# Three vector-matrix products of layer 0 issued in single steps instead of in three bursts

## The chip, the cores and the metric

The kernel runs on one core of a Trainium2 chip, in one launch. The metric is the time of an execution on the device, in microseconds (us). The engines are named as in the profile: PE (TensorE, matrix products; PEld is its weight load), DVE (VectorE), ACT (ScalarE), POOL (GpSimd) and SP (SyncE, here only the queue that issues the transfers from HBM).

## The reference, cut to what matters

Two layers, each an attention-like mixer and an MLP, on x of 1024 tokens by 1024 columns, all in float32. Ahead of each layer, six vectors of 1024 are made from the one conditioning vector c:

```
cond = silu(c)
mod  = cond @ w_ada[l] + b_ada[l]          # 6 * 1024
shift_a, scale_a, gate_a, shift_f, scale_f, gate_f = split(mod, 6)
h = rms_norm(x) * (1 + scale_a) + shift_a
x = x + gate_a * mixer(h)                  # gated linear attention and latent attention
h = rms_norm(x) * (1 + scale_f) + shift_f
x = x + gate_f * (relu(h @ w_up)**2 @ w_down)
```

The vectors are numbered 0 to 5 here and called modulations. The change concerns 2 (gate_a), 3 (shift_f) and 4 (scale_f) of layer 0. None of them is needed before the mixer's output projection, which stands far behind the work that is spoken of here.

## The kernel before, in words

Activations lie transposed, columns on partitions, in two halves (A and B) of 512 tokens. Float32 products are made as three matmuls of a high and a low part each. So each weight block of 512 KB is loaded into a ring slot (SP queue), its high part is cast (ACT or DVE, L307), its low part subtracted (POOL or DVE, L308), and PE uses both.

All large buffers are slots of 4 KB per partition of one pool of 51, the ring. A slot that is given back goes to the end of a first-in-first-out list, and the next request takes the head of the list (class `Arena`). A load into a slot may be issued only when the last reader of its previous tenant is done, and SP issues its transfers in one fixed order.

The stages of a layer are tokens of the string PROGRAM, walked in order at build time, once for each layer. For half A and then half B: v0, v1, g0, g1 (value and gate projections), L (latent projection, with latent_rest behind it), Q or TA/QA and TB/QB (queries and keys, and the latent's rest), W (the seven-level scores of gated linear attention: PE L928 and DVE L954 to L989), O (their output); R makes the rotary tables: a chain of small DVE steps in one slot `ang`, that ends with ACT's sine and cosine (L551 to L556). The tile framework takes the dependencies of this walk and sets from them, and from a planned time for each engine, the order in which each engine gets its instructions. The engines then run each its own list in order, with semaphores between them.

One modulation is `ada_steps` (L240): for each of 8 blocks of w_ada a load of 512 KB (L245) and one DVE step over 128x1024 that multiplies it by an entry of cond and adds it up (L254 the first, L256 the others). One load is requested a step ahead of its use. The last step also makes eight PE transposes of the sum (L263) and four short DVE operations (L266, L267), with one more each for modulation 4. `ada` (L236) runs all eight steps at once; token Xm calls it.

Names in the rows: s is a ring tile, ps_x, ps_s, ps_m, ps_g are PSUM banks, tmp a small buffer, colsv and mod hold columns of vectors, cs the constants. L609 to L611 (L607 to L609 in the changed kernel) are the three matmuls of a value or gate projection.

Of the kernel before, what the change touches and what calls it, by code (L numbers as in the profile page):

```python
# [34 lines left out]


PROGRAM = (
# [3 lines left out]
).split()  # L41
# [85 lines left out]
def hybrid_kernel(  # L127
# [17 lines left out]
    R = lambda a: a.bitcast(F32R)  # L145
# [86 lines left out]
    def mcol(l, m, d):  # L232
        k = l * 48 + m * 8 + d
        return mod[:, k:k + 1]

    def ada(l, m):  # L236
        for _ in ada_steps(l, m):
            pass

    def ada_steps(l, m, tag=lambda: "x"):  # L240
        acc = AR.alloc()
# [77 lines left out]
    def ahead(n):  # L319
        while ustate["pos"] < min(n, len(units)) and len(AR.free_list) >= 5:  # L320
            prep()
# [19 lines left out]
    for l in range(DEPTH):  # L341
# [10 lines left out]
        for tok in PROGRAM:  # L352
            kind, rest = tok[0], tok[1:]
# [228 lines left out]
    def rope(dst, src, i, hf, room):  # L582
        C = ropeC[i][:, hf * 4:hf * 4 + 4, :]
        Sn = ropeS[i][:, hf * 4:hf * 4 + 4, :]
        m1 = room[:, 0:256].rearrange("p (t f) -> p t f", t=4)
        m2 = room[:, 256:512].rearrange("p (t f) -> p t f", t=4)
        G.tensor_tensor(m1, src, C, op=ALU.mult)
        G.tensor_tensor(m2[:, :, 0:32], src[:, :, 32:64], Sn[:, :, 0:32], op=ALU.mult)
        G.tensor_tensor(m2[:, :, 32:64], src[:, :, 0:32], Sn[:, :, 32:64], op=ALU.mult)
        G.tensor_tensor(dst[:, :, 0, :], m1, m2, op=ALU.add)  # L590
        G.tensor_tensor(dst[:, :, 1, :], m1, m2, op=ALU.add)


    wg = cp.tile([32, 256], F32, name="wg")
# [20 lines left out]
    def layer_mixer(l, hA, make_hB):  # L615
# [498 lines left out]
        def flush():  # L1114
            while pending:
                pending.pop(0)()
# [20 lines left out]
        for tok in PROGRAM:  # L1137
            kind, rest = tok[0], tok[1:]
            hf = "AB".index(rest[0]) if rest and rest[0] in "AB" else None
            if kind == "L":  # L1140
                latents(hf)
            elif kind == "H":
                hsb[1] = (hsb[1] or []) + make_hB(rest)
            elif kind == "R":
                if l == 0:
                    rope_angles()
                rope_tables(l)
            elif kind == "E":
                if l == 0:
                    enter(1)  # L1150
            elif kind == "T":
                latent_rest(hf)
            elif kind == "Q":
                queries_keys(hf)
            elif kind == "W":
                gla_scores(hf)
            elif kind == "v":
                values(hf, int(rest[1]))
            elif kind == "g":
                gates(hf, int(rest[1]))  # L1160
            elif kind == "O":
                gla_out(hf)
            elif kind == "M":
                mix_split(int(rest))
            elif kind in "uU":
                up(tok)
            elif kind == "a":
                attend(int(rest[0]), int(rest[1]))
            elif kind == "F":
                flush()  # L1170
            elif kind == "=":
                tags = TAGS[rest]
            elif kind == "X":
                if l == 0:
                    ada(0, int(rest))
            elif kind == "P":
                ahead(ustate["pos"] + int(rest))
            elif kind == "D":
                project(0, int(rest), mix)
                if int(rest) == 7:  # L1180
                    AR.free(*mix[0])
            elif kind == "N":
                norm_out(0)
# [274 lines left out]
```

## Time and profile before

| what | value |
|---|---|
| three runs | 2352.49, 2353.1, 2366.69 us (median 2353.1) |
| profiled execution | 2356.47 us, its span 2354.4 us |
| PE busy | 2236.2 us (95%) |
| DVE busy | 1810.4 us (77%) |
| ACT busy | 1141.1 us (48%) |
| POOL busy | 453.5 us (19%) |
| one percent of the median | 23.5 us |

The span is that from the first instruction of the profiled execution to its last; 2.07 us of its time lie around it. A busy share is that of the whole span. An idle time in square brackets, as `[3.05 <-DVE s L256]`, stands just ahead of the row that it belongs to, with the operation that ended it.

### The profile page before, as it was taken

The numbers are of one execution on the slowest core, as the hardware profiler recorded it, in microseconds if no ns is written. First come the engines' busy times: TensorE is split into PE (matmuls) and PEld (weight loads), VectorE is DVE, ScalarE is ACT, GpSimd is POOL, SyncE is SP. The second block draws the span as 40 slices with busy tenths as digits, with TensorE's granted clock in tenths as the row PEclk, the third lists the DMA queues.
The fourth block names the chain that finished last, engine by engine and source line by source line (L and its number), as shares of the span: only waits on it lengthen the run. The fifth ranks groups of instructions, "written<-read, shape, count | busy, mean of one in ns | idle before, by whom it ended". The sixth has DMA issues, their size and how long they took to land.

```text
span 2354.4 us, 30787 instructions
## 1 busy us (share of the span) xinstructions
PE 2236.2 (95%) x11784; PEld 1897.1 (81%) x11784; DVE 1810.4 (77%) x2453; ACT 1141.1 (48%) x1764; POOL 453.5 (19%) x326
## 2 busy tenths in 40 slices
PE   6999999899999998998989999899999999999999
PEld 4788888788788876887878889788888878887887
DVE  5897867857888888989995757786674767877894
ACT  3364746534732383433444556575366217733432
POOL 2452642420030000000063355333102000000000
PEclk8999999999999999999999999999999999999999
DMA  9633100136668655765641211003454564375562
GB/s 345 205 97 99 55 27 10 46 125 212 199 206 274 217 167 174 249 225 197 239 131 45 70 51 41 10 10 100 144 169 124 180 202 146 110 237 189 163 212 81
DMA packets 244855, 340.51 MB, mean 145 GB/s; under 512 B 11078, under 2 KB 166884, under 8 KB 244708
## 3 DMA queue, kind: packets, MB, share of 16 engines
q1 hardware_dynamic: 244160, 338.08, 44.2%
q8 instruction: 92, 1.51, 0.3%
q10 hardware_dynamic: 548, 0.48, 0.1%
q14 instruction: 55, 0.45, 0.1%
HBM read 317.54 MB, written 20.97 MB: 144 GB/s over the span
## 4 chain that ended last, share of the span: by engine, by line
PE 63%; DVE 12%; DMA 7%; ACT 2%; issue 2%; POOL 1%; SPq 0%; DVEq 0%; ACTq 0%; POOLq 0%
PE ps_m L162 8%; PE ps_m L163 7%; PE ps_m L161 7%; PE ps_s L162 5%; PE ps_s L163 5%; PE ps_s L161 5%; PE ps_g L163 4%; PE ps_g L162 4%; PE ps_g L161 4%; DMA s<-in_w_mlp_down_dram 3%; PE ps_x L163 2%; PE ps_x L162 2%; PE ps_x L161 2%; DMA s<-in_w_mlp_up_dram 2%; DMA s<-in_w_ada_dram 1%
## 5 line engine op out<-in xcount | busy, mean ns | idle before, releaser
L307 ACT CAST s<-s 128x1024 fp32r<-128x1024 f32 (+2 forms) x306 | 315.2, 1035 | 465.5 <-DVE s L304 275.7
L162 PE MATMUL ps_m<-s,s 128*128 128x512 f32 (+3 forms) x1084 | 411.1, 380 | 15.2 <-DVE s L1292 14.2
L308 POOL TENSOR_TENSOR s<-s,s 128x1024 fp32r<-128x1024 f32 (+2 forms) x90 | 222.7, 2481 | 1044.9 <-DVE s L307 524.1
L161 PE MATMUL ps_m<-s,s 128*128 128x512 f32 (+3 forms) x1084 | 408.6, 381 | 8.6 <-ACT s L1291 5.4
L163 PE MATMUL ps_m<-s,s 128*128 128x512 f32 (+3 forms) x1084 | 408.3, 377 | 0.2 <-DVE s L308 0.2
L308 DVE TENSOR_TENSOR s<-s,s 128x1024 fp32r<-128x1024 f32 (+1 forms) x224 | 272.5, 1227 | 55.6 <-ACT s L307 47.6
L161 PE MATMUL ps_s<-s,s 128*128 128x512 f32 (+5 forms) x800 | 306.4, 387 | 6.6 <-ACT s L724 6.1
L163 PE MATMUL ps_s<-s,s 128*128 128x512 f32 (+5 forms) x800 | 305.3, 383 | 1.5 <-DVE s L308 1.5
L162 PE MATMUL ps_s<-s,s 128*128 128x512 f32 (+5 forms) x800 | 305.2, 382 | 0.5 <-DVE s L748 0.5
L304 DVE TENSOR_TENSOR s<-s,s 128x1024 f32<-128x1024 f32 x160 | 196.9, 1233 | 122.1 <-DMA s<-in_w_mlp_up_dram 77.6
L162 PEld LDWEIGHTS ps_m<-s,s 128*128 128x128 f32 x1084 | 206.4, 190 | 55.9 <-DVE s L1292 17.7
L161 PEld LDWEIGHTS ps_m<-s,s 128*128 128x128 f32 x1084 | 205.6, 190 | 46.5 <-ACT s L1291 7.4
L1291 ACT CAST s<-s 128x1024 fp32r<-128x1024 f32 x140 | 146.7, 1051 | 192.8 <-DVE s L1289 57.2
L163 PEld LDWEIGHTS ps_m<-s,s 128*128 128x128 f32 x1084 | 206.0, 190 | 35.8 <-DVE s L308 0.6
L162 PE MATMUL ps_g<-s,s 128*128 128x512 f32 (+1 forms) x506 | 195.0, 386 | 1.6 <-DVE s L1292 1.6
L161 PE MATMUL ps_g<-s,s 128*128 128x512 f32 (+1 forms) x506 | 194.6, 388 | 0.8 <-DVE s L1338 0.8
L163 PE MATMUL ps_g<-s,s 128*128 128x512 f32 (+1 forms) x506 | 194.3, 387 | 0.8 <-DVE s L308 0.8
L1292 DVE TENSOR_TENSOR s<-s,s 128x1024 fp32r<-128x1024 f32 x140 | 173.5, 1244 | 13.8 <-ACT s L1291 10.8
L161 PEld LDWEIGHTS ps_s<-s,s 128*128 128x128 f32 x800 | 150.8, 189 | 37.0 <-ACT s L724 8.7
L163 PEld LDWEIGHTS ps_s<-s,s 128*128 128x128 f32 x800 | 151.4, 189 | 30.9 <-DVE s L308 1.9
L162 PEld LDWEIGHTS ps_s<-s,s 128*128 128x128 f32 x800 | 151.6, 190 | 27.6 <-DVE s L748 0.7
L162 PE MATMUL ps_x<-s,s 128*128 128x512 f32 (+3 forms) x362 | 124.1, 344 | 0.0
(332 smaller groups left out, 4412.6 us busy)
## 6 DMA issues: line engine op xcount, KB each, us to landing
s<-in_w_mlp_up_dram SPq DMA_DIRECT2D x192, 512.0 KB, 4.9
s<-in_w_mlp_down_dram SPq DMA_DIRECT2D x192, 512.0 KB, 4.3
s<-in_w_ada_dram SPq DMA_DIRECT2D x80, 512.0 KB, 4.8
s<-in_w_in_dram SPq DMA_DIRECT2D x48, 512.0 KB, 3.9
s<-in_w_ada_dram SPq DMA_DIRECT2D x32, 256.0 KB, 4.6
xd<-s SPq DMA_DIRECT2D x16, 512.0 KB, 6.1
s<-in_w_out_dram SPq DMA_DIRECT2D x16, 512.0 KB, 4.5
s<-xd SPq DMA_DIRECT2D x16, 512.0 KB, 3.5
```

The lines of the kernel that those rows point to most:

```text
L161: PE.matmul(o, lh, rh, start=start, stop=False)
L162: PE.matmul(o, lh, rl, start=False, stop=False)
L163: PE.matmul(o, ll, rh, start=False, stop=stop)
L304: V.tensor_tensor(raw[:, :n], raw[:, :n], u.second[:, :n], op=ALU.add if u.sign > 0 else ALU.subtract)
L307: (V.tensor_copy if u.eng[-2] == "v" else S.copy)(R(u.hi[:, :n]), raw[:, :n])
L308: (V if u.eng[-1] == "v" else G).tensor_tensor(R(u.lo[:, :n]), raw[:, :n], u.hi[:, :n], op=ALU.subtract)
L1291: S.copy(R(hi), t)
L1292: V.tensor_tensor(R(lo), t, hi, op=ALU.subtract)
```

## The change

The token X2, X3 and X4 each ran a whole modulation. Now the token Xn takes n steps from one generator that runs through modulations 2, 3 and 4 one after the other. Twelve tokens X2 stand between the stages of the mixer, from behind `=1` up to gB1: 24 steps, as many as before. The helper `ada` is gone. Layer 1 takes none, as before.

```diff
 PROGRAM = (
-    "vA0 E gA0 X2 R LA Ha =1 TA QA X3 Hb vA1 WA gA1 OA LB QB TB X4 gB0 WB gB1 u00 P1 vB0 u01 a00 P1 "
+    "vA0 E gA0 R LA Ha =1 X2 TA X2 QA X2 Hb vA1 X2 WA X2 gA1 X2 OA X2 LB X2 QB X2 TB X2 gB0 X2 WB X2 gB1 u00 P1 vB0 u01 a00 P1 "
...
-    def ada(l, m):
-        for _ in ada_steps(l, m):
-            pass
...
+    ada_work0 = (None for m in (2, 3, 4) for _ in ada_steps(0, m))
...
             elif kind == "X":
                 if l == 0:
-                    ada(0, int(rest))
+                    for _ in range(int(rest)):
+                        next(ada_work0)
```

Lines 240 to 590 of the kernel before are four lines further up in the changed one, later ones two. The tiles of the ring are numbered differently in the two, since the requests come in another order.

The first place is PE's list at the transposes of modulation 2 (L263 before, L259 now). Before, they stand within the latent projection of half A (128x464 matmuls):

```order
L161 MATMUL ps_s<-s_106_823,s_73_405 128x464
L161 MATMUL ps_m<-s_106_823,s_73_405 128x464
L161 MATMUL ps_s<-s_106_823,s_73_405 128x464
L263 MATMUL ps_x<-cs,s_91_729 128x128 x8
L162 MATMUL ps_s<-s_107_824,s_73_405 128x464
L163 MATMUL ps_s<-s_106_823,s_73_405 128x464
```

In the changed kernel they stand two stages later, between the halves of value projection vA1 and the first of the scores (L926):

```order
L607 MATMUL ps_s<-s_132_1072,s_39_298 128x256
L608 MATMUL ps_s<-s_133_1073,s_39_298 128x256
L609 MATMUL ps_s<-s_132_1072,s_39_298 128x256
L259 MATMUL ps_x<-cs,s_112_928 128x128 x3
L607 MATMUL ps_m<-s_135_1104,s_71_395 128x256
L607 MATMUL ps_s<-s_135_1104,s_71_395 128x256
L259 MATMUL ps_x<-cs,s_112_928 128x128
L926 MATMUL ps_g<-s_157_1331,s_127_1036 128x128
```

Those of modulation 3 move from ahead of the scores of half A to behind its latent stage LB, those of modulation 4 behind projection gB0.

The second place is DVE's list at the end of the rotary angles. Before:

```order
L551 TENSOR_SCALAR s_100_770<-s_100_770 128x256
L553 TENSOR_SCALAR s_100_770<-s_100_770 128x256
L554 TENSOR_TENSOR s_100_770<-s_100_770 128x256
L579 SCALAR_TENSOR_TENSOR s_102_806<-sinT,grp 128x8x32 x2
L839 COPY s_79_424<-ps_x 16x512
L555 TENSOR_SCALAR s_100_770<-s_100_770 128x256
L857 TENSOR_REDUCE ssq<-s_123_997 128x2 x3
L392 TENSOR_SCALAR rs_v<-ssq 128x4 x3
```

In the changed kernel (L551 there is L555 of before, L837 is L839, L252 is L256):

```order
L551 TENSOR_SCALAR s_91_729<-s_91_729 128x256
L252 SCALAR_TENSOR_TENSOR s_112_928<-s_114_931,cond,s_112_928 128x1024
L855 TENSOR_REDUCE ssq<-s_117_960 128x2 x3
L252 SCALAR_TENSOR_TENSOR s_112_928<-s_115_934,cond,s_112_928 128x1024
L303 CAST s_132_1072<-s_131_1070 128x1024
L855 TENSOR_REDUCE ssq<-s_118_965 128x2 x3
L252 SCALAR_TENSOR_TENSOR s_112_928<-s_124_1029,cond,s_112_928 128x1024
L388 TENSOR_SCALAR rs_v<-ssq 128x4 x3
L837 COPY s_79_424<-ps_x 16x512
```

Three steps of modulation 2 now stand between the last of the angles and the copy (L837) that PE's decay product waits for, and block s_114_931 of the first of them is loaded into the slot in which the angles (s_91_729) lay.

The third place is SP's list around the first block of gate projection gB0, which is s_200_1980 in both. Before:

```order
L292 DMA s_189_1881<-in_w_in_dram 128x8x128
L292 DMA s_197_1948<-in_w_in_dram 128x8x128
L292 DMA s_192_1911<-in_w_in_dram 128x8x128
L292 DMA s_200_1980<-in_w_in_dram 128x4x256
L245 DMA s_221_2176<-in_w_ada_dram 128x1024
L245 DMA s_218_2168<-in_w_ada_dram 128x1024
```

In the changed kernel:

```order
L288 DMA s_248_2578<-in_w_in_dram 128x4x256
L288 DMA s_245_2524<-in_w_in_dram 128x4x256
L241 DMA s_231_2309<-in_w_ada_dram 128x1024
L241 DMA s_232_2312<-in_w_ada_dram 128x1024
L288 DMA s_200_1980<-in_w_in_dram 128x4x256
L241 DMA s_244_2500<-in_w_ada_dram 128x1024
```

The block was row 87 of SP's list and is now row 103. It comes behind the two rows ahead of it in w_in of later use (s_248, s_245) and behind two blocks of modulation 4. Its slot is now that of a tile which the output stage of half A reads to its end (PE L1085 there).

## Rows read from the trace of the kernel before

**Rows 1.** The page's busy times of each engine over the span.
```profile
PE 2236.2 (95%) x11784; PEld 1897.1 (81%) x11784; DVE 1810.4 (77%) x2453; ACT 1141.1 (48%) x1764; POOL 453.5 (19%) x326
```
**Rows 2.** Stretches: us, PE PEld DVE ACT POOL busy, TensorE clock, DMA share.
```profile
50.00:100.00 50.00, 45.55 (x278) 42.15 (x279) 41.80 (x56) 22.15 (x36) 15.67 (x7) 0.90 0.61 216
...
150.00:200.00 50.00, 43.36 (x273) 40.14 (x272) 43.90 (x58) 26.41 (x43) 18.04 (x14) 0.93 0.30 84
200.00:250.00 50.00, 50.00 (x276) 43.04 (x275) 32.30 (x62) 24.98 (x43) 17.25 (x16) 0.97 0.40 123
```
**Rows 3.** Waits of PE, 45 to 460 us: in total, times, longest.
```profile
PE ps_x L263 <- DVE s L256: 6.6, 2, 3.6
```
**Rows 4.** Timeline of PE at the first burst: start, us, operation, [idle before].
```profile
89.78 1.09 PE L263 MATMUL ps_x<-cs,s 128*128 128x128 f32 x8 [3.05 <-DVE s L256]
...
91.03 0.59 PE L163 MATMUL ps_s<-s,s 128*128 128x464 f32 x1
91.42 0.59 PE L161 MATMUL ps_s<-s,s 128*128 128x464 f32 x1
...
94.38 0.37 PE L162 MATMUL ps_s<-s,s 128*128 128x464 f32 x1
94.58 0.38 PE L161 MATMUL ps_m<-s,s 128*128 128x464 f32 x1
```
**Rows 5.** Timeline of PE at the second burst.
```profile
154.69 1.07 PE L263 MATMUL ps_x<-cs,s 128*128 128x128 f32 x8 [3.55 <-DVE s L256]
...
155.76 0.42 PE L609 MATMUL ps_m<-s,s 128*128 128x256 f32 x1
155.98 0.42 PE L610 MATMUL ps_m<-s,s 128*128 128x256 f32 x1
...
160.24 0.28 PE L610 MATMUL ps_m<-s,s 128*128 128x256 f32 x1
160.36 0.28 PE L611 MATMUL ps_m<-s,s 128*128 128x256 f32 x1
```
**Rows 6.** Stretches of 5 us at the first burst, columns as in rows 2.
```profile
85.00:90.00 5.00, 1.95 (x11) 1.44 (x10) 5.00 (x6) 2.70 (x4) 1.50 (x2) 1.00 0.00 0
90.00:95.00 5.00, 5.00 (x21) 4.40 (x20) 5.00 (x7) 1.08 (x3) 1.96 (x1) 0.66 0.00 0
```
**Rows 7.** Timeline of DVE at the end of the rotary angles.
```profile
114.43 0.27 DVE L555 TENSOR_SCALAR s<-s 128x256 f32<-128x256 f32 x1
117.45 1.21 DVE L857 TENSOR_REDUCE ssq<-s 128x2 f32<-128x512 f32 x3 [2.75 <-ACT s L855]
...
120.51 0.17 DVE L395 SCALAR_TENSOR_TENSOR rs_a<-rs_y 128x12 f32<-128x12 f32 x1 [1.64 <-ACT rs_y L394]
```
**Rows 8.** Timeline of ACT at the same place.
```profile
114.73 0.42 ACT L556 ACTIVATE cosT<-s 128x256 f32<-128x256 f32 x1 [2.42 <-DVE s L555]
```
**Rows 9.** Transfers: landing of L245's blocks, then issues of the page (KB, us).
```profile
DMA to landing us min/median/max: 3.8/4.8/9.8
...
s<-in_w_in_dram SPq DMA_DIRECT2D x48, 512.0 KB, 3.9
```
**Rows 10.** Timeline of PE at the decay product.
```profile
114.55 1.98 PE L843 MATMUL ps_x<-s,wg 17*128 17x512 f32 x4 [1.58 <-DVE s L839]
```
**Rows 11.** Timeline of SP: blocks of w_in issued ahead of LB and gB0.
```profile
137.15 30.13 SPq L292 DMA_DIRECT2D s<-in_w_in_dram  x7
```
**Rows 12.** The page's group of casts: busy, mean ns, idle before.
```profile
L307 ACT CAST s<-s 128x1024 fp32r<-128x1024 f32 (+2 forms) x306 | 315.2, 1035 | 465.5 <-DVE s L304 275.7
```
**Rows 13.** Timeline of DVE ahead of the scores of half B.
```profile
242.62 0.69 DVE L848 SCALAR_TENSOR_TENSOR s<-ps_x,tmp 128x512 f32<-128x512 f32 x1 [4.92 <-ACT tmp L847]
```
**Rows 14.** Timeline of DVE in the first burst.
```profile
78.10 1.27 DVE L256 SCALAR_TENSOR_TENSOR s<-s,cond,s 128x1024 f32<-128x1024 f32 x1
...
80.56 3.44 DVE L256 SCALAR_TENSOR_TENSOR s<-s,cond,s 128x1024 f32<-128x1024 f32 x1
```
**Rows 15.** Timeline of POOL in the same stretch.
```profile
80.53 5.53 POOL L308 TENSOR_TENSOR s<-s,s 128x1024 fp32r<-128x1024 f32 x2 [2.90 <-ACT s L307]
```

## The prediction, made before the changed kernel had run

> **What bounds the kernel now.** I read the page first, then the stretches, then PE's waits, then the timelines where a wait stood. PE is busy for 95% of the span [rows 1], so only time in which PE stands, or runs at its lower clock, can be won or lost. The edit reorders work between about 45 and 460 us; from about 560 us on each engine's list is the same but for one exchange. In that part PE is short of full by 4.45 us between 50 and 100, by 6.64 between 150 and 200, and not at all between 200 and 250 [rows 2]. DVE is the busy neighbour: 43.90 of 50 us at 150 to 200, but only 32.30 at 200 to 250.
>
> The sums go against the profiled execution, 2356.47 us. It lies 3.4 us above the median of 2353.1, to which I carry the difference. From no change this kernel can tell about 1%, or 23.5 us.
>
> **What is removed.** PE waits for a burst's DVE steps twice, 6.6 us in all [rows 3]: 3.05 us ahead of modulation 2's transposes and 3.55 ahead of modulation 3's [rows 4, 5]. Nothing of modulation 4 is in that row, so its burst already lay beside other work. In the 5 us with the first wait PE was busy for 1.95; in the next 5 the granted clock was 0.66, a mix of the lower level (1.2 GHz) and the full one [rows 6]. The timelines show what that cost. From 89.78 to 94.38, 4.60 us, matmuls start 0.39 us apart instead of 0.20 [rows 4]: 4.60 x (1 - 0.20/0.39) = 2.2 us. From 154.69 to 160.24, 5.55 us, they start 0.22 apart instead of 0.12 [rows 5]: 2.5 us. So at most 6.6 + 4.7 = **11.3 us** can come back. In the changed order the transposes stand where their sums are made early, so I take it all.
>
> **What is added.** The work is the same: 24 blocks, 24 DVE steps, 24 transposes, as many additions. The string only costs where a step, its load or its slot is late for what stands behind it. I followed each list for such places and found three.
>
> *The end of the angles.* The first moved step of modulation 2 in this place needs a block that is loaded into the slot of the angles. That slot is free when ACT has made the cosine, which reads it last: DVE's last step starts at 114.43, ACT's ends at 114.73 + 0.42 = 115.15 [rows 7, 8]. Only then can SP issue the load, and it lands a median 4.8 us later, 3.8 at least [rows 9]. So DVE stands at that step for about 0.4 + 4.8 = 5.2 us. Before, it stood there for 2.75 + 1.64 = 4.39 us anyway, for ACT [rows 7]; that hides much of DVE's loss. It doesn't hide PE's: the copy that its decay product waits for, which stood ahead of the last angle step, now stands behind the late step and two others of 1.27 us [rows 14]. PE waited 1.58 us for that copy [rows 10]. Now the copy comes at least 5.2 + 2 x 1.27 = 7.7 us behind the angles. PE has other matmuls ahead of that product, some of which start later as well now that the burst no longer delays them, so between nothing and about 6 us of this are new wait or half clock; I take 4, which is the late step less what the old wait of 1.58 hides (5.2 - 1.58 = 3.6), with something for the clock.
>
> *The latent projection of half B.* SP had issued seven blocks from 137.15 on, over 30.13 us, well ahead of LB [rows 11]. Now the second and third blocks of LB take slots that the last readers of the scores of half A hold, so their loads are issued when these end. The rest of O is too short for a load of 3.9 us [rows 9], a cast of 1.04 [rows 12] and the low part. That it is hidden altogether gives 0; that it is exposed but for the cast gives 3.9 + 1.04 = 4.9, say 5. I take 2.75, near the middle, because some transposes of O still cover it.
>
> *The first block of gate projection gB0.* It was loaded with those seven [rows 11], and PE had no wait there: 50.00 of 50 us [rows 2]. Now it goes into a slot that the last transposes of O of half A read, and stands in SP's list behind two blocks of modulation 4 and two later ones of w_in. Counted from the release: landing 3.9 [rows 9], cast 1.04 [rows 12], issue about 0.4, less 1.3 for the few small matmuls that PE still has: 4.0 us of standing at least, and 2 at the lower clock if that follows as it did at the bursts. If SP stands at one of the rows ahead first, which takes another landing (4.8 [rows 9]), it is up to 9 + 2 = 11. I don't let it be free, since no order of release lets the block land early; I take **6**, from 2 to 11. DVE's idle time there, 4.92 us [rows 13], is behind PE's gate matmuls before and so pays nothing.
>
> Modulation 4's last step may be late by up to 1 us at its transposes; I count 0. In the stretch behind, DVE has some steps fewer, and PE's remaining waits there are on the score steps; I count 0 too.
>
> **Sum:** -11.3 + 4 + 2.75 + 6 = +1.5 us. The ends are -11.3 + 0 + 0 + 2 = -9 and -11.3 + 6 + 5 + 11 = +11. On the median that is 2354.6, from 2344 to 2364: **no change that can be measured**.
>
> At one point a rule speaks against the change. In the first burst a step of 1.27 us took 3.44 while POOL ran two subtractions, 5.53 us, from the same moment [rows 14, 15]. The Trainium skill, "SBUF — State Buffer", section "SBUF: two separate sides", says that a DVE instruction with two SBUF inputs and a GpSimd instruction that reads SBUF share a port pair, and that the one that starts second blocks until the first has finished. The trace agrees in kind: the step ends about 0.7 us behind the middle of the pair. By that rule more steps could meet POOL when they are spread into stages in which it works; this is rival C.
>
> **Rival A: nothing takes the place of the waits.** For it speaks that DVE and DMA have room at 200 to 250 us (32.30 of 50 busy, DMA 0.40 [rows 2]). Against it: three loads that now wait for a slot. Time: 2353.1 - 11.3 = 2341.8.
>
> **Rival B, the other side: the loads of the ring come one behind the other.** At gB0 SP's list is in order. If the row of w_in ahead waits for a modulation step on DVE, and that step for its own block, then gB0's block comes two landings behind the release, not one. PE stands for 9 + 4.8 = 13.8 us or so, with 2 for the clock; the other places take their upper ends, 6 and 5, and one more block of modulation 4 is late by 1. Sum: -11.3 + 16 + 6 + 5 + 1 = +16.7, hence about 2370. It decides against the change once gB0's block is issued more than about 4 us behind the last O transpose. For it: the slot order is first in, first out, so 24 requests that stand between others move everybody's slot. Against it: the DMA engines are idle for 60% of that stretch [rows 2].
>
> **Rival C: the spread steps meet POOL.** A step that does takes 3.44 - 1.27 = 2.17 us more [rows 14]. POOL works for 18.04 of 50 us at 150 to 200 [rows 2]. Were all of seven steps in the scores of half A met, that is 15.2 us on a DVE with 50 - 43.90 = 6.1 us to spare [rows 2]: 9.1 on PE's path, since the score matmuls wait for DVE. With the terms of the sum: +1.5 + 9.1 = +10.6, or 2363.7. Against it: in the burst itself it struck few steps.
>
> **Rival D: the edit moves nothing that PE sees.** Then 2353. Against it: both transposes that PE waited for stand elsewhere.
>
> **How the numbers follow.** My forecast gets 0.52, A 0.18, B 0.18, C 0.08, D 0.04. The predicted time is that of the forecast, 2354.6. The range goes from A's 2342 to B's 2370, and leaves out about 2 in 10, of A and of B beyond these ends. The likeliest case alone is 2344 to 2364. More than 1% faster would need 2329.6, twice what the bursts cost PE; I give 0.03 for waits beyond these that go too. More than 1% slower needs 2376.6, B and C together: 0.06. The rest, 0.91, is within 1%.
>
> **What would show it.** Right: no wait of PE for a modulation step ahead of its transposes of modulations 2 and 3; a DVE idle of about 5 us for a transfer just behind the last angle step; a wait of PE of 4 to 9 us at the first matmuls of gB0, and one of 2 to 4 in LB, with a low granted clock just behind them; equal timelines from 560 us on, shifted by one amount. Wrong: PE with no new gap at gB0 (A), SP standing in front of gB0's block for 10 us or more (B), or several steps of 3 us and over in the scores (C). A shift that goes on growing behind 560 us would overturn the claim that the lists there are alike.

## The result and the profile after

The changed kernel takes 2371.57 us in the median of 7 runs (2364.48 to 2379.65), the kernel before 2353.1 of 7. The ratio is 1.0074, its 95% interval 1.0048 to 1.0099. The change is slower, by less than the 1% that I had named as the bound of a measurable one, but clear of the noise and 1.6 us beyond the end of the forecast's range.

The profiled execution, 2364.48 us, was the shortest of the seven, so its span (2362.7 us, against 2354.4) shows 8.3 us of a difference that is about twice that. Over the runs that went with the experiments, 93 of the kernel before, and all 13 of the changed one, the medians are 2356.6 and 2371.6. At one mean granted clock they are as far apart: at 0.978 the means are 2358.4 (20 runs) and 2373.0 (4), at 0.980 2355.7 (19) and 2371.6 (2). So some 15 us have to be found, and the mean clock is not where they are.

The page of the changed kernel, busy time of each engine: PE's work is that of before [rows 1] but for 1.2 us, and DVE does not do more either.

```profile
span 2362.7 us, 30778 instructions
...
PE 2237.4 (95%) x11784; PEld 1897.7 (80%) x11784; DVE 1793.5 (76%) x2453; ACT 1142.5 (48%) x1764; POOL 457.6 (19%) x326
```

The stretches of the changed kernel, in the columns of [rows 2]:

```profile
150.00:200.00 50.00, 39.49 (x246) 35.18 (x245) 46.59 (x54) 27.53 (x45) 18.15 (x12) 0.93 0.43 132
200.00:250.00 50.00, 42.47 (x206) 34.45 (x205) 32.96 (x62) 18.83 (x35) 20.33 (x16) 0.96 0.41 126
245.00:250.00 5.00, 0.00 (x0) 0.00 (x0) 0.39 (x1) 1.63 (x4) 1.01 (x2) 0.58 1.00 346
```

Against [rows 2] PE lost 3.87 us between 150 and 200 (39.49 for 43.36) and 7.53 between 200 and 250 (42.47 for 50.00). Both waits of [rows 4, 5] are gone, and PE's waits of this part now read as follows (three of them; waits of PE, 45 to 460 us; in total, times, longest):

```profile
PE ps_x L867 <- DVE s L846: 7.7, 2, 7.0
PE ps_g L926 <- DVE s L987: 7.4, 5, 2.1
...
PE ps_x L476 <- DVE s L468: 3.1, 1, 3.1
```

L867 are the transposes of half B's latents ahead of gB0, L926 the score matmuls, L476 spreads the reciprocal norms of half B's tokens over the partitions. The first wait on PE's timeline, what DVE did in it, and what SP issued:

```profile
243.44 1.09 PE L1085 MATMUL ps_g<-cs,s 128*128 128x128 f32 x8
251.56 1.11 PE L867 MATMUL ps_x<-cs,s 128*128 128x128 f32 x4 [7.02 <-DVE s L846]
...
254.69 0.41 PE L607 MATMUL ps_m<-s,s 128*128 128x256 f32 x1
254.90 0.41 PE L608 MATMUL ps_m<-s,s 128*128 128x256 f32 x1
```

```profile
249.61 1.28 DVE L252 SCALAR_TENSOR_TENSOR s<-s,cond,s 128x1024 f32<-128x1024 f32 x1 [6.50 <-DMA s<-in_w_ada_dram]
250.81 0.68 DVE L846 SCALAR_TENSOR_TENSOR s<-ps_x,tmp 128x512 f32<-128x512 f32 x1
```

```profile
241.45 1.77 SPq L288 DMA_DIRECT2D s<-in_w_in_dram  x2
243.31 0.93 SPq L241 DMA_DIRECT2D s<-in_w_ada_dram  x2
244.35 0.38 SPq L288 DMA_DIRECT2D s<-in_w_in_dram  x1
```

Read from the bottom. SP stands from 235.68 to 241.45, since its next row is a block of w_in whose slot a step of modulation 4 reads until 241.42. Then five blocks go within 3 us: two of w_in, the two of modulation 4 from 243.31 on, and at 244.35 the first of gB0, directly behind, which is the third place of the order shown ahead of the prediction. From 245 to 250 the DMA engines are full (1.00, 346 GB/s, in the last row of the stretches). The first block of modulation 4 is there at 249.6, 6.3 us after its issue, where the median was 4.8 [rows 9]. DVE has stood 6.50 us for it, and the copy L846 that PE's transposes need stands behind that step. PE stands 7.02 us and then runs at half rate (matmuls of 256 columns 0.21 us apart, 0.12 in [rows 5]).

The third wait of the list stands where the prediction had not looked, ahead of the first burst's place. The timelines of PE, DVE and POOL there:

```profile
73.24 1.16 PE L476 MATMUL ps_x<-cs,tmp 128*128 128x128 f32 x8 [3.06 <-DVE s L468]
```

```profile
65.31 1.92 DVE L391 SCALAR_TENSOR_TENSOR rs_a<-rs_y 128x4 f32<-128x4 f32 x1
67.26 2.10 DVE L392 TENSOR_TENSOR rs_a<-rs_a,rs_v 128x4 f32<-128x4 f32 x1
69.39 2.29 DVE L393 SCALAR_TENSOR_TENSOR rst<-rs_a,rs_y 128x4 f32<-128x4 f32 x1
```

```profile
62.66 8.99 POOL L304 TENSOR_TENSOR s<-s,s 128x928 fp32r<-128x928 f32 x4 [3.98 <-ACT s L303]
```

Three operations over four columns take 6.3 us, each until one of POOL's four subtractions ends (67.20, 69.33 and 71.65), and the copy L468 that PE needs stands behind them. In the kernel before POOL makes one subtraction there and is done at 64.33, and the same three take 0.15 or 0.16 us each:

```profile
64.79 0.15 DVE L395 SCALAR_TENSOR_TENSOR rs_a<-rs_y 128x4 f32<-128x4 f32 x1
```

All eleven traces of kernels with modulation 2 in single steps and its blocks in the ring have this wait (3.05 to 3.08 us). The six with its burst at the old place, or seven steps of it, do not have it.

**Where the lag arises.** For the table I gave each matmul the usual time from its start to the next one's start (the 15th percentile of its kind in the traces compared), added them up in the order of execution, and took how much later than in the kernel before the same amount of PE's work is reached. The columns are the time in the kernel before. Minus is ahead.

```
kernel          153 us  202 us  222 us  246 us  314 us  572 us
changed           -3.5     4.4     4.4    15.1    14.6     9.4
again             -2.5     4.5     4.4    15.5    14.6    14.6
m4_burst          -4.4     3.6     3.6     6.2     3.6     7.7
m23_burst          0.7     3.7     3.6     7.1     5.9     6.4
one_load          -2.8     1.3     1.4     5.7     2.1     2.1
late_end          -1.0     2.0     2.0     0.1     2.8     0.1
scores_free       -1.6    -0.2     0.5     5.1    10.0    13.8
two_ahead         -3.1    -1.4    -1.4    12.5     8.6     3.6
no_late           -3.1     5.0     5.0    15.1    22.7    18.1
light3            -0.5    -6.3    -6.4    -6.0    -1.2    -1.2
mod3_late         -1.2    -5.8    -5.8    -6.2    -6.0    -1.6
rot_before         0.2    -2.8    -2.9     2.7     6.6     6.4
rot_after         -3.4     7.7     8.2     6.2     8.4     7.3
rot_after6        -3.3     6.1     6.3     4.1    20.4    24.2
rot_two           -1.2     6.2     6.4     4.7     4.6     8.1
own_before         6.0    15.8    15.8    13.9    23.6    28.4
own_after         -4.8     9.2     9.1     7.3    16.1    20.6
```

The column of 153 us lies inside the kernel before's second wait (151.14 to 154.69), so it holds neither all of the bursts' gain nor the gain alone. The same reckoning in finer stretches, with one usual time for each shape of matmul (it agrees with the table within about 2 us; the numbers are gains and losses inside a stretch, minus is a gain):

```
kernel       0-66  66-84  84-98  98-150  150-156  156-202  202-222  222-246
changed       0.5    3.5   -5.2     0.6     -3.9      8.9      0.2     10.1
again         0.8    5.0   -5.2     0.8     -3.9      7.3      0.2     10.5
m23_burst     0.9    0.0    0.0     0.0      0.3      3.0      0.2      2.8
late_end     -1.1    0.5   -3.0     3.3     -0.4      2.9      0.0     -1.8
own_before    0.7    0.1   -4.0    13.1     -2.0      9.2      0.0     -2.2
own_after     0.6    0.5   -5.2     5.1     -3.9     12.7      0.1     -1.9
```

In the changed kernel PE loses 3.5 us at L476, wins 5.2 and 3.9 where the two waits stood, loses 8.9 in the scores of half A and 10.1 around gB0.

### The profile page after: what moved, and what is told of

Same layout as the page of the kernel before. It is cut to its first block, busy times and chain, and to the rows that moved or that the text cites. A ratio compares the mean times of both kernels' runs of the same rounds, so it can differ in the third digit from the quotient of the medians.

```text
span 2362.7 us, 30778 instructions
## 1 busy us (share of the span) xinstructions
PE 2237.4 (95%) x11784; PEld 1897.7 (80%) x11784; DVE 1793.5 (76%) x2453; ACT 1142.5 (48%) x1764; POOL 457.6 (19%) x326
## 4 chain that ended last, share of the span: by engine, by line
PE 48%; DVE 8%; DMA 4%; ACT 1%; issue 1%; POOL 1%; SPq 0%; DVEq 0%; ACTq 0%; POOLq 0%
PE ps_m L162 5%; PE ps_m L163 5%; PE ps_m L161 5%; PE ps_s L162 4%; PE ps_s L163 4%; PE ps_s L161 4%; PE ps_g L163 3%; PE ps_g L162 3%; PE ps_g L161 3%; DMA s<-in_w_mlp_down_dram 2%; PE ps_x L163 2%; PE ps_x L162 2%; PE ps_x L161 2%; DMA s<-in_w_in_dram 1%; DVE s L304 1%
## 5 line engine op out<-in xcount | busy, mean ns | idle before, releaser
L162 PE MATMUL ps_m<-s,s 128*128 128x512 f32 (+3 forms) x1084 | 410.5, 379 | 14.6 <-DVE s L1291 13.7
```

Of the source, the lines that this page charges most:

```text
L162: PE.matmul(o, lh, rl, start=False, stop=False)
```

## The experiments

Theory 1 was that single steps lose by blocks that come late, rival 2 that DVE's steps in the scores cost, rival 3 that the granted clock of single executions makes the difference.

**again**: the changed kernel, no edit.

> The changed kernel unchanged, for a second profile. Its profiled execution was the fastest of seven (2364.5 us, the median 2371.6). If the loss lies at fixed places of the program (theory 1, gate projection gB0), the profile shows PE standing about 7 us ahead of the latent transposes of half B again, and the time is 2364 to 2378, ratio 1.004 to 1.010. If the loss lies in the granted clock of single executions (rival 3), a slower profile has the same waits and longer stretches at the lower level.

Measured: 2370.9 us, ratio 1.0059 (1.0041 to 1.0076). The wait is there again:

```profile
251.05 1.11 PE L867 MATMUL ps_x<-cs,s 128*128 128x128 f32 x4 [6.62 <-DVE s L846]
```

The table's two rows agree within 1 us up to 314 us. Behind it this execution keeps its 14.6 us, and the other one falls to 9.4, with the same lists of PE and DVE. So the loss arises by 246 us; what comes after is scatter between executions, in which rival 3 is right.

**m4_burst** and **m23_burst**: one part of the change each.

```diff
-... LB X2 QB X2 TB X2 gB0 X2 WB X2 gB1          (the changed kernel)
+... LB X2 QB TB X8 gB0 WB gB1                   (m4_burst)
+vA0 E gA0 X8 R LA Ha =1 TA QA X8 Hb vA1 WA gA1 OA LB X2 QB X2 TB X2 gB0 X2 WB gB1   (m23_burst)
```

> Modulations 2 and 3 in single steps, modulation 4 as one burst at its old place. Theory 1 (a block of modulation 4 is late, DVE stands for it in front of the copies that PE's latent transposes wait for, and PE stands 7.0 us and then runs about 10 us at the lower clock): that wait is gone, 7 to 12 us come back, ratio 0.998 to 1.003. Rival 2 (the steps of modulations 2 and 3 in the scores of half A, where DVE is full): little comes back, ratio 1.005 to 1.008.

> Modulations 2 and 3 as bursts at their old places, modulation 4 in single steps from LB to WB. Theory 1: the wait of about 7 us at the latent transposes of half B stays and the bursts' 11.3 us are not won, ratio 1.003 to 1.010. Rival 2: the scores of half A are as before, and the time is that of before, ratio 0.999 to 1.002.

Measured: m4_burst 2369.78 us, 1.0058 (1.0041 to 1.0075); m23_burst 2367.48, 1.0046 (1.0029 to 1.0063). In m4_burst the wait at L867 is gone, and the lag at 246 us falls from 15.1 to 6.2, as theory 1 said. But the time fell by hardly 1 us, outside theory 1's range and in rival 2's: the other part had been lost in the scores already, and the execution lost 4 more by 572 us. In m23_burst the time is theory 1's and the wait is not: 1.1 us, not 7, though modulation 4 is in single steps. So single steps of modulation 4 alone don't make it, and yet either part alone costs half a per cent. Of m23_burst's lag 3.0 us arise in the scores, where its steps are those of the kernel before: so not all that is lost there needs steps that were moved into it.

**one_load**: one block of eight loaded for each modulation of layer 0; the other seven are left out.

```diff
-            if k < 7:
+            if k < 7 and l:
                 coming = load(k + 1)
...
-            AR.free(raw)
+            if l or k == 7:
+                AR.free(raw)
```

> Single steps as in the changed kernel, but only the first of a modulation's eight blocks is loaded in layer 0 and used for all eight steps (the seven other blocks are left out); the DVE steps, transposes and their places in the program stay. Theory 1 (late blocks, and the slots that their requests move): no step is late, and the 11.3 us of the bursts are won in part: 2342 to 2352, ratio 0.995 to 0.999. Rival 2 (DVE's steps in the scores): the loss in the scores stays, ratio 1.002 to 1.005.

Measured: 2363.38 us, 1.0036 (1.0023 to 1.005). Both missed. Most of the lag at 314 us is gone (2.1 for 14.6) with as many DVE steps, which speaks for loads and slots, but the kernel is not faster than before.

**late_end**: bursts of seven steps at their old places, the step with the transposes later.

```diff
-vA0 E gA0 X2 R LA Ha =1 TA QA X3 Hb vA1 WA gA1 OA ...     (before: X2, X3 are bursts of 8)
+vA0 E gA0 X7 R LA Ha =1 X1 TA QA X7 Hb vA1 WA gA1 X1 OA LB QB TB X8 gB0 WB gB1
```

> Modulations 2 and 3 as bursts of seven steps at their old places, so that loads, slots and DVE steps stay there, and only the eighth step (with the transposes that PE waited for) is taken later: that of modulation 2 behind =1, that of modulation 3 behind gA1; modulation 4 as before. Theory 1 (the bursts cost PE only what it waits for their transposes, and single steps lose by late blocks): 4 to 11 us are won over the kernel before, ratio 0.995 to 0.999. Rival 2 (in this stretch PE waits for DVE's total work, so a wait that is removed at the transposes comes back in the scores): ratio 0.999 to 1.002.

Measured: 2359.93 us, 1.0016 (0.9999 to 1.0033). Rival 2's number. The waits for the transposes, 3.05 and 3.55 us [rows 4, 5], are gone, and these stand in the next places where PE needs DVE, the decay product (1.58 before [rows 10]), the first scores (L926) and, later, the gates (L1041):

```profile
112.32 3.48 PE L841 MATMUL ps_x<-s,wg 17*128 17x512 f32 x4 [3.39 <-DVE s L837]
...
154.79 1.44 PE L926 MATMUL ps_g<-s,s 128*128 128x128 f32 x5 [3.04 <-DVE s L952]
...
178.38 0.76 PE L161 MATMUL ps_s<-s,s 128*128 128x464 f32 x1 [2.95 <-DVE s L1041]
```

Here the waits for DVE, which is busy for 43.90 of 50 us [rows 2], moved on when only the waiting instruction was moved. The 3.0 us that PE wins between 84 and 98 us are given back by 150.

**light3** and **mod3_late**: the kernel before with less DVE work at that place. light3 cuts seven steps of modulation 3 to 64 columns (the rest is left out); mod3_late moves its burst behind OB.

```diff
+                w = 64 if (l, m) == (0, 3) else 1024
-                V.scalar_tensor_tensor(acc, raw, cond[:, k:k + 1], acc, op0=ALU.mult, op1=ALU.add)
+                V.scalar_tensor_tensor(acc[:, 0:w], raw[:, 0:w], cond[:, k:k + 1], acc[:, 0:w], op0=ALU.mult, op1=ALU.add)
```

```diff
-... QA X3 Hb vA1 WA gA1 OA LB QB TB X4 ... vB1 OB =2 ...
+... QA Hb vA1 WA gA1 OA LB QB TB X4 ... vB1 OB X3 =2 ...
```

> The kernel before, with the last seven DVE steps of modulation 3 of layer 0 cut to 64 of 1024 columns (the rest of the sum is left out); loads, slots and transposes stay. Some 8 us of DVE's work between 137 and 155 us are gone. Rival 2: PE's waits for DVE there fall by as much, 3.55 us at the transposes and some of the half clock behind them, and do not come back in the scores: 5 to 9 us less, ratio 0.996 to 0.998. Theory 1 as first put (only the wait for the transposes costs): 3 to 6 us.

> The kernel before, with the burst of modulation 3 moved from half A's scores to behind OB, where DVE is busy for 30 to 34 of 50 us. Rival 2: the 10 us of DVE's work are out of the stretch in which PE waits for it, 4 to 9 us less, ratio 0.996 to 0.998, if no load is late behind it. Theory 1 in its second form: the other requests shift, and any load of the ring may be late in return: 0.997 to 1.005.

Measured: light3 2355.64 us, 1.0000 (0.9987 to 1.0014); mod3_late 2357.3, 1.0003 (0.9986 to 1.0019). Neither gains, so both miss rival 2's ratio, and light3 theory 1's too. Both are ahead by about 6 us at 202 us, the lead that rival 2 asked for, and give most of it back: light3 by 314 us, mod3_late by 572. The stretches of light3 show it:

```profile
150.00:200.00 50.00, 49.40 (x342) 46.65 (x342) 37.83 (x54) 30.93 (x50) 16.03 (x11) 1.00 0.33 98
200.00:250.00 50.00, 46.22 (x275) 39.90 (x274) 34.65 (x61) 22.66 (x41) 21.76 (x17) 1.00 0.37 117
```

PE has 6.04 us more than in [rows 2] between 150 and 200 and 3.78 less between 200 and 250. So even without most of a burst's work on DVE the time is the same at the end: a lead of PE of some 6 us does not survive half B's stages. The lists behind the cut are not those of before, though. The framework plans anew with the shorter steps, and at 143 of DVE's 2453 places, nearly all between 140 and 332 us, light3 has another operation than the kernel before. What eats the lead, DVE's load or that order, these two runs do not separate.

**scores_free**, **two_ahead**, **no_late**: three ways to take theory 1's late blocks, or rival 2's steps, away.

```diff
+... vA1 X2 WA gA1 OA X3 LB X3 QB X3 TB X3 gB0 X2 WB X2 gB1     (scores_free)
+... OA X2 LB X2 QB TB gB0 X4 WB X4 gB1                         (no_late)
+        coming = [load(0), load(1)] if l == 0 else [load(0)]   (two_ahead)
...
+            raw = coming.pop(0)
+            n = k + (2 if l == 0 else 1)
+            if n < 8:
+                coming.append(load(n))
```

> Single steps, but the four that stood behind gA1 and in the scores of half A come in threes from OA on. Rival 2 (DVE's steps in the scores): the scores of half A need 3 to 8 us less on PE than in the changed kernel, ratio 1.002 to 1.005 to the kernel before. Theory 1 (late blocks): the scores lose only the part that stands for a late block, and gB0 is the place that decides: 1.004 to 1.009.

> Single steps as in the changed kernel, but each block of layer 0's modulations is requested two steps ahead of its use instead of one (one slot more in use). Theory 1 (the blocks come late): DVE's waits for blocks (37.9 us in 22 places in the changed kernel's trace) fall by half or more, and PE's wait of 7 us ahead of the latent transposes of half B goes: ratio 0.999 to 1.004. If it is the ring's other requests that are late, because the spread steps take their slots, the wait moves to another load and the ratio stays at 1.005 to 1.009.

> Single steps up to QB, none from there to gB0, then four behind gB0 and four behind WB. Theory 1: no block of modulation 4 stands ahead of the copies for the latent transposes of half B, the wait of 7 us is gone, and PE's lag to the kernel before at that place falls from 14 us to 4 to 7: ratio 1.002 to 1.005. Rival 3 (the loss is in the granted clock of the stretches behind): the time stays at 1.005 to 1.008 with that wait gone.

Measured: scores_free 2372.14 us, 1.0062 (1.0042 to 1.0081); two_ahead 2373.08, 1.0062 (1.004 to 1.0084); no_late 2380.16, 1.0094 (1.0075 to 1.0114). scores_free is in theory 1's range and not in rival 2's, no_late is in no range, and two_ahead is beyond theory 1's first range and in the second. scores_free and two_ahead repair the scores (lag -0.2 and -1.4 at 202 us for 4.4), as rival 2 said of scores_free, and lose it again by 314 and 246 us. two_ahead did what it was built for. The 37.9 us in 22 places of its expectation are those of the whole trace; 24.5 of them, in 17 places, lie in layer 1, where the edit changes nothing. In layer 0 (up to 460 us) DVE's idle time for blocks falls from 13.4 us to 7.0; first the changed kernel, then two_ahead:

```profile
  DMA s<-in_w_ada_dram: 13.4, 5
  DMA s<-in_w_ada_dram: 7.0, 5
```

PE's wait of 7 us for L846 (here L847) is 2.0 us. PE now waits in the latent projection of half B, for a cast and a low part of w_in (ACT stands 1.64 and 1.05 us for two of its blocks):

```profile
235.26 0.79 PE L163 MATMUL ps_s<-s,s 128*128 128x512 f32 x1 [2.57 <-DVE s L305]
```

That is the other branch of what was expected, in place and in ratio: another load is late.

In no_late PE's wait is unchanged. The timelines of PE, ACT, DVE and SP:

```profile
252.51 1.97 PE L867 MATMUL ps_x<-cs,s 128*128 128x128 f32 x8 [6.92 <-DVE s L846]
```

```profile
246.99 1.04 ACT L303 CAST s<-s 128x1024 fp32r<-128x1024 f32 x1 [3.71 <-DMA s<-in_w_in_dram]
247.94 1.08 ACT L843 ACTIVATE tmp<-ps_x 128x512 f32<-128x512 f32 x2
```

```profile
238.30 0.74 DVE L250 TENSOR_SCALAR s<-s,cond 128x1024 f32<-128x1024 f32 x1
...
244.26 3.92 DVE L252 SCALAR_TENSOR_TENSOR s<-s,cond,s 128x1024 f32<-128x1024 f32 x3 [3.30 <-DMA s<-in_w_ada_dram]
```

```profile
227.55 12.81 SPq L241 DMA_DIRECT2D s<-in_w_ada_dram  x5
240.46 5.32 SPq L288 DMA_DIRECT2D s<-in_w_in_dram  x2
```

The string has modulation 4 behind gB0, but the lists do not: the framework put five of its steps ahead of L846, the first of them L250 at 238.30. So the premise that no block of modulation 4 stands ahead did not hold, and the run does not test it. The late block is one of w_in: SP issues it at 240.46, behind three blocks of modulation 4 from 239.07 on, and it is there at 246.99. ACT stands in its cast, and L843, from which L846 is made, stands behind. From these runs theory 1 took its second form: what is late is whatever block of the ring falls upon a slot that is held long or stands behind others in SP's list, and the spread requests change which.

**own_before** and **own_after**: the blocks and sums of layer 0's modulations in three tiles of their own, in either kernel.

```diff
-NSLOT = 51
+NSLOT = 48
...
-        acc = AR.alloc()
+        acc = AR.alloc() if l else own1.tile([P, 1024], F32, tag="acc0", name="acc0")
...
-            raw = AR.alloc()
+            raw = AR.alloc() if l else own.tile([P, 1024], F32, tag="raw0", name="raw0")
```

> The kernel before, but the blocks and sums of layer 0's modulations lie in three tiles of their own, outside the ring, which has 48 slots instead of 51. It is the partner of own_after. A ring with fewer slots may cost something of its own: ratio 0.998 to 1.006 to the kernel before, on both theories.

> The changed kernel with the same three tiles of their own and 48 slots: the spread requests no longer move any other slot. Theory 1 in its second form (the spread requests shift the ring, so that some block, of a modulation or of w_in, comes late around gB0): PE's wait of about 7 us ahead of the latent transposes of half B is gone, and the ratio to own_before is 0.996 to 1.001. Rival 2 (in this part PE waits for DVE's total of work, so that neither order wins, and the scores lose with single steps): 1.002 to 1.006 to own_before.

Measured: own_before 2465.07 us, 1.0467 (1.0448 to 1.0486); own_after 2456.02, 1.0432 (1.0413 to 1.0451). Three slots fewer cost 4%, far more than I had expected, most of it from 900 us on. Of the pair, the single steps are the faster: 2456.02 / 2465.07 = 0.9963. Without their requests in the ring they win 9 us, theory 1's number, and there is no loss around gB0 (lag 9.1 at 222 us, 7.3 at 246), but own_before has none there either. The win comes from another place than theory 1 said. By the finer stretches own_before is 9.9 us behind the kernel before at 150 us, own_after 1.0; between 156 and 202 us own_after loses 12.7 us and own_before 9.2. So in the scores single steps lose 3.5 us more even with their requests outside the ring, which speaks for rival 2 there.

**rot_before**, **rot_after**, **rot_after6**, **rot_two**, **rot_two4**: in the program nothing but the ring's free list is turned, once or twice, in either kernel.

```diff
+            elif kind == "K":
+                if l == 0:
+                    for _ in range(int(rest)):
+                        AR.free_list.append(AR.free_list.pop(0))
...
-... OA LB QB TB X4 ...                 +... OA K2 LB QB TB X4 ...             (rot_before)
-... OA X2 LB X2 QB ...                 +... OA X2 K4 LB X2 QB ...             (rot_after; K6: rot_after6)
-... Hb vA1 X2 WA ... OA X2 LB ...      +... Hb K3 vA1 X2 WA ... OA X2 K2 LB   (rot_two; K4, K2: rot_two4)
```

> The kernel before, bursts and all, with one thing added: ahead of LB the ring's free list is turned by two places (two slots go from its head to its end), so that the same requests get other slots. No step, load or transpose is added or moved in the program. The first block of gB0 then lies in a slot that the output stage of half A reads late, as in the changed kernel. Theory 1 in its second form (what costs is which slot a block of w_in gets): PE waits at gB0 or ahead of the latent transposes of half B, 5 to 15 us, ratio 1.002 to 1.006. Rival (the moved steps themselves cost): ratio 0.999 to 1.001.

> The changed kernel with the free list turned by four places ahead of LB. The first block of gB0 then needs a slot that is free once a step of modulation 3 is done, long before the output stage ends. Theory 1 in its second form: PE's wait of 7 us is gone or another request is late in its place; if none is, 6 to 12 us less than the changed kernel, ratio 0.999 to 1.004. Rival (the moved steps themselves cost): as the changed kernel, 1.005 to 1.008.

> As rot_after, by six places: both blocks of gB0 need slots that are free when LB's low parts are made. Theory 1 in its second form: 0.998 to 1.004, and a time that differs from rot_after by several us though the program is the same. Rival: 1.005 to 1.008 for both.

> The changed kernel with the free list turned by three places ahead of vA1 and by two ahead of LB, so that both the first block of LB (late in the scores of half A) and the first block of gB0 (late behind the output stage) need slots that are free early. Theory 1 in its second form: neither DVE's wait of 3.9 us at the low part in the scores nor PE's of 7 us at gB0 is left, PE's lag to the kernel before at 180 us of its work falls from 15 us to between -4 and 3: ratio 0.997 to 1.002. Rival (DVE's steps in the scores cost by themselves): the lag in the scores of 4 to 8 us stays, ratio 1.002 to 1.005.

> As rot_two, but turned by four places ahead of vA1. Both theories as for rot_two: 0.997 to 1.002 if the slots are what costs, 1.002 to 1.005 if DVE's steps are.

Measured: rot_before 2367.19 us, 1.0031 (1.0017 to 1.0046); rot_after 2368.93, 1.0042 (1.0028 to 1.0055); rot_after6 2385.17, 1.0109 (1.0092 to 1.0127); rot_two 2365.61, 1.0049 (1.0029 to 1.0069); rot_two4 2378.07, 1.0089 (1.0066 to 1.0111).

No token is moved, but the lists are. From other slots follow other dependencies, and the framework orders each list anew: at 160 of DVE's 2453 places, between 162 and 348 us, rot_before has another operation than the kernel before, at 293 places rot_after another than the changed kernel (again: at none). So a turn shows what the slots do together with the order that is made from them.

rot_before has the bursts and every step where it was in the program. The turn alone makes it slower, by theory 1's ratio but at another place: a wait of PE in the output stage that the kernel before has nothing of at this place:

```profile
238.34 1.33 PE L1087 MATMUL ps_g<-cs,s 128*128 128x128 f32 x5 [5.54 <-DVE s L1082]
```

DVE and POOL ahead of it in rot_before, and DVE in the kernel before:

```profile
229.91 7.65 DVE L865 TENSOR_TENSOR s<-s,rst 128x512 f32<-128x512 f32 x6
...
230.88 2.83 POOL L308 TENSOR_TENSOR s<-s,s 128x1024 fp32r<-128x1024 f32 x1
...
234.90 2.51 POOL L308 TENSOR_TENSOR s<-s,s 128x1024 fp32r<-128x1024 f32 x1
```

```profile
231.41 2.46 DVE L865 TENSOR_TENSOR s<-s,rst 128x512 f32<-128x512 f32 x6
```

Two low parts of w_in now fall on POOL beside DVE's six L865, which take 5.2 us more than in the kernel before. Here most of the price is paid where DVE and POOL meet.

In rot_after the first block of gB0 was given a slot that is free early. The wait at L867 is gone, and PE is full where it lost 7.53 us:

```profile
200.00:250.00 50.00, 50.00 (x287) 43.35 (x286) 32.13 (x68) 21.04 (x39) 15.38 (x16) 1.00 0.27 81
```

The lag does not grow at gB0 (8.2 to 6.2), while the changed kernel's grows by 10.7. Its ratio is just past theory 1's range. The loss at this place is not the price of single steps as such: slots and the order made from them decide it. Which of the two, the run leaves open, since DVE's list has both copies L846 ahead of the next step of modulation 4 now:

```profile
241.18 0.69 DVE L846 SCALAR_TENSOR_TENSOR s<-ps_x,tmp 128x512 f32<-128x512 f32 x1 [0.83 <-ACT tmp L845]
...
252.81 1.29 DVE L252 SCALAR_TENSOR_TENSOR s<-s,cond,s 128x1024 f32<-128x1024 f32 x1 [1.11 <-DMA s<-in_w_ada_dram]
```

rot_after6 has the same string but for the number of places turned and is 16 us slower; it misses both ranges. The four turns of the changed kernel lie from 1.0042 to 1.0109, around its own 1.0059 and 1.0074, and the one of the kernel before at 1.0031. So the choice of slots moves the time by as much as the whole change does, but no turn of the single steps was as fast as the bursts.

For the scores the last two runs were meant to decide, and did not. In the changed kernel DVE stands there for the cast of LB's first block:

```profile
144.49 1.12 DVE L304 TENSOR_TENSOR s<-s,s 128x928 fp32r<-128x928 f32 x1 [3.93 <-ACT s L303]
```

In rot_two that block is early, but DVE stands in the same place for something else, and the lag stays at 6.2, with a ratio that is the rival's (1.0049):

```profile
148.43 0.75 DVE L250 TENSOR_SCALAR s<-s,cond 128x1024 f32<-128x1024 f32 x1 [4.57 <-issue]
```

rot_two4, at 1.0089, is in neither range (by the finer reckoning it is 9.9 us behind at 202 us and 15.4 at 314). How much of the loss in the scores is a late block, how much the three steps of modulation 3 at 147 to 154 us and how much the new order of DVE's list stays open. No kernel here beats the one before.

## Why the prediction was wrong, point by point

**The step that failed: "The string only costs where a step, its load or its slot is late ... I followed each list for such places and found three."** With that, all other places were put at nothing. The changed kernel lost 3.5 us at L476, a place without a moved step, and 8.9 us in the scores of half A: 12.4 us for which the sum has no term. The third term, gB0, was mis-sized besides: 10.1 to 10.7 us for 6. The paragraphs on gB0, the scores and L476 below say what the runs showed there; why the scores lose so much stays open.

**What is removed: -11.3 us, "so I take it all".** The price was right at its places, and the gain did not last. PE wins 5.2 us between 84 and 98 us, where 3.05 + 2.2 had been forecast, and 3.9 between 150 and 156, the second wait of 3.55; the 2.5 for the half clock behind it fall into the scores, where PE waits again. late_end shows that the step does not hold by itself: without the two waits, and with the bursts' other seven steps in place, the ratio is 1.0016, as the waits came back at the next places. light3 and mod3_late lead by 6 us at 202 us and end at 1.0000 and 1.0003. I had measured the cost of a wait at the wait, and not asked what PE would wait for next.

**The end of the angles: +4.** The mechanism was right and the price wrong. DVE stood 4.53 us for the block, 5.2 forecast:

```profile
103.48 1.28 DVE L252 SCALAR_TENSOR_TENSOR s<-s,cond,s 128x1024 f32<-128x1024 f32 x1 [4.53 <-DMA s<-in_w_ada_dram]
...
112.28 1.12 PE L841 MATMUL ps_x<-s,wg 17*128 17x512 f32 x2 [1.19 <-DVE s L837]
```

But PE waited 1.19 us for the copy, 1.58 before [rows 10]: the matmuls in front of it covered the rest. The term was about 0, its lower end.

**The latent projection of half B: +2.75.** PE's wait for the cast in LB was 0.54 us. Near the lower end again.

```profile
191.36 0.48 PE L161 MATMUL ps_m<-s,s 128*128 128x464 f32 x1 [0.54 <-ACT s L303]
```

**The first block of gB0: +6, from 2 to 11.** Place and chain were right, the size at the upper end: 10.7 us. The wait ended not in gB0's own matmuls but before them, in the transposes, since DVE stood in its list for a block of modulation 4 that SP had issued just ahead. Rival B's chain was there in its first half: SP was held for 5.8 us by a row of w_in, until a modulation step on DVE was done, and issued five rows from 241.45 on. The blocks then came beside one another, not one behind the other, and the DMA engines, which the prediction had found 60% idle in [rows 2], were full from 245 to 250 us (1.00). Rival B's 2370 is the nearest of all the times on record, and that is luck: it has 16 us at gB0, 11 at the angles and LB, where nothing was lost, and none in the scores.

**What was not in the sum: the scores, +8.9.** I had counted the seven steps there as hidden unless POOL met them (rival C), and had not looked for the cast of LB's first block in ACT's and DVE's lists. As rival C's price this loss does not come out. DVE's score steps took up to 1.8 us there, where 0.68 is their usual time, but so did some in the kernel before. What DVE's operations took beyond their usual time between 140 and 185 us (the time of the same operation and shape elsewhere in the traces) adds up to about 10.6 us in the changed kernel and 8.5 in the kernel before: 2.1 us of difference. No step took 3 us there, the longest 2.32.

**What was not in the sum: L476, +3.5.** Here rival C's mechanism decided, with other instructions than the moved steps: DVE's three operations of 0.15 us each took 6.3 beside POOL, and PE stood 3.06 us. The rule of the Trainium skill on the shared port pair ("SBUF — State Buffer", section "SBUF: two separate sides") fits these rows: each of the three has two inputs in SBUF and ends within 0.04 us of the end of a subtraction on POOL.

**The sum.** By the finer stretches 0.5 + 3.5 - 5.2 + 0.6 - 3.9 + 8.9 + 0.2 + 10.1 = +14.7 us, against +1.5. Rival A's time was not seen: the waits went, and others stood in other places. "No change that can be measured" was wrong in the mean, as 13 runs against 93 resolve 15 us well.

**The trace behind 560 us** was to be shifted by one amount. It is so only but for the scatter between executions: the two are 9.4 and 14.6 us behind at 572 us and 8.3 and 18.6 at the end of their spans, with the same lists of PE and DVE.

## What to carry to other kernels

Where slots come from a first-in-first-out ring, an interleaved request is never only its own work: it hands later loads other slots, and one that falls upon a tile that is read long can stall every in-order list that it stands in. Follow the loads of the kernel's own weights through the new order, not only those of the moved work, and turn the ring as a control before crediting or blaming the moved steps. Compare the lists of such a control operation by operation, too: where a framework orders them, an edit of one thing reorders others, and a step can run where its token does not stand. See what runs on POOL beside DVE in the new order, even beside DVE's smallest operations. And price a removed wait by what the waiting engine needs next: in late_end the waits came back at the next places, and in light3 a lead of 6 us was gone by 314 us.

## What was not expected of the hardware

Two executions of one program with the same waits up to 314 us differ by 5 us at 572, and runs of the kernel before take 2353.7 us in the mean at a mean granted clock of 0.982 (9 runs) and 2362.0 at 0.977 (10). So 0.005 in the mean clock goes with 8 us here, as much as the span's difference that the first pair of profiles showed. One profile of each kernel would have sized this change at half of what it costs.

Three DVE operations over 128x4 took 1.92, 2.10 and 2.29 us beside POOL's subtractions, for 0.15 or 0.16 each without them: on DVE an operation's size did not bound its time.
